# Queueing the sums of weights behind the low parts that precede them

## The chip, the cores and the metric

The kernel runs on one core of a Trainium2 chip. A core has a matrix engine, TensorE (PE in the profile), three engines for elementwise work, VectorE (DVE), ScalarE (ACT) and GpSimd (POOL), and a queue engine, SyncE (SP), that issues most transfers from HBM. Each engine works through its own instructions in program order and waits on semaphores for the others. The metric is the time of one execution on the device, in microseconds (us), as the median of several runs.

## The reference

Two layers, each a mixer between two half-step SwiGLU FFNs, over 512 tokens of width 1024, all in float32. The first layer's mixer is a gated linear attention, the second's a stick-breaking attention. The four FFNs are where the change acts.

```python
D_MODEL, SEQ, DEPTH, D_FF = 1024, 512, 2, 2816

def swiglu(h, w_gate, w_up, w_down):
    return (jax.nn.silu(h @ w_gate) * (h @ w_up)) @ w_down

def reference(x, ffn1_norm, ...):
    for i in range(DEPTH):
        x = x + 0.5 * swiglu(rmsnorm(x, ffn1_norm[i]), ffn1_w_gate[i], ffn1_w_up[i], ffn1_w_down[i])
        h = rmsnorm(x, mix_norm[i])
        ...
        x = x + y.astype(x.dtype)
        x = x + 0.5 * swiglu(rmsnorm(x, ffn2_norm[i]), ffn2_w_gate[i], ffn2_w_up[i], ffn2_w_down[i])
    return rmsnorm(x, final_norm)
```

## The kernel before

**Products in three.** Every operand of a matrix product is split into two parts that PE takes at full speed: a high part, which ScalarE makes by a cast (`wh` for weights, L126), and a low part, which VectorE makes by subtracting the high part from the original (`wl`, L127). One float32 product is then three on PE: high by high, low by high, high by low. For an activation the two parts are called `hh` and `hl`, `nh` and `nl`, `th` and `tl` (L788, L789).

**Blocks of seven products.** Most of the FFNs' products are done in two-by-two blocks with seven block products in place of eight. `seven` (L667) does it for the gate and up projections, `seven_down` (L333) for a part of the down projection. The scheme needs sums of weight blocks: four VectorE additions per block of weights, `s12` and `s34`. In `seven` they are L677 and L678 (`s12`) and L683 and L684 (`s34`), 72 of each; in `seven_down` they are L353, L354, L360 and L361, 16 of each. A sum is itself a weight: it gets a high and a low part.

**Entries, views, splits.** The weights that a step needs are an `Entry`: units of a chunk of raw weights (`raw`, `rawd`), a view of it, and a body, a generator that issues the PE work. A seven-product block is two entries: the first has two raw blocks (`ax`, a11 and the one that goes with b21) and `s12`, the second has `s34` and the raw block a22. `Entry.view` loads the chunk and calls the view: for a raw block that is a slice without an instruction, for a sum it issues the two VectorE additions. `Entry.split` then issues, for each unit, the cast L126 and the subtraction L127. `Feed.start` runs ahead of the entry i that begins: it splits entries i to i+2, views entries up to i+3, and loads the chunks up to i+5.

**Who decides the order.** The instructions are traced in the order of that program, and a scheduler then places them on each engine's queue; `tc.issue_after(x)` makes the instructions traced inside it come later than x in the queue. It adds an order, not a wait.

**What follows the products.** In `seven`'s two bodies PE fills the banks `ps_w`, `ps_q` and `ps_z`. ScalarE copies intermediate sums out (`z` L718, `o1` L721, `o0` L724, `u3` L736), VectorE adds (L737, L740), and in the up projection multiplies by the gate (L707). The products L707 from `ps_z` and `ps_w` also empty those banks. The result is cut into `hh` (L788) and `hl` (L789), the inputs of the down projection.

**The down projection.** An FFN's 11 columns of 256 hidden features come in six groups; groups 1 and 3 go through `seven_down`, in two parts each, 0 and 1, so there are four such blocks in an FFN and 16 in all. Part 0 follows right on the last up pair of its group. Its first body does the products a11 by b11 into `ps_w`, copies them into `ps_z` (L387, ScalarE), then t1 into `ps_q`, t2 on top of `ps_w`, b21 on top of `ps_z`, and adds each into the residual `x` on VectorE (L375). The second body adds t3 on top of `ps_w`, which therefore waits until L375 has added the former content of `ps_w` into x0 and x1.

**Buffers.** The low parts `wl` rotate over four buffers, and so do the high parts and the sums; a low part waits until PE has used the one whose place it takes. The raw weights have two.

Of the kernel before, what the change touches and what calls it, by code (L numbers as in the profile page):

```python
# [10 lines left out]
F32 = mybir.dt.float32  # L11
# [4 lines left out]
ALU = mybir.AluOpType  # L16
# [16 lines left out]
def decoder(ctx: ExitStack, tc: tile.TileContext, a: dict, out: bass.AP):  # L33
    nc = tc.nc
# [59 lines left out]
    class Entry:  # L94
# [7 lines left out]

        def view(self):

            if self.views is None:
                self.views = [view(ch.load()) for ch, view, _, _ in self.units]
            return self.views

        def split(self):
            if self.W is None:  # L110
                self.W = []
                for r, (_, _, n, m) in zip(self.view(), self.units):
                    few = n * m < 1024
                    if few:

                        h = st["few"].tile([P, n * m + NEAR], F32R, tag="vh", bufs=1, name="wh")[:, NEAR:]
                        l = st["few"].tile([P, n * m + 64 - NEAR], F32R, tag="vl", bufs=1, name="wl")[:, : n * m]
                    else:
                        h, l = (
                            wp.tile([P, n * m + 64], F32R, tag="w" + t, bufs=4, name="w" + t)[  # L120
                                :, self.place : self.place + n * m
                            ]
                            for t in "hl"
                        )
                    h, l = (t.rearrange("p (n m) -> p n m", m=m) for t in (h, l))
                    st["cut"] = nc.scalar.copy(h, r).ins  # L126
                    nc.vector.tensor_tensor(out=l, in0=r, in1=h.bitcast(F32), op=ALU.subtract)  # L127
                    self.W.append((h, l))
                    if self.lead and len(self.W) == 1:


                        first = wp.tile([P, P], F32R, tag="w1", bufs=1, name="w1")
                        with tc.issue_after(st["cut"]):
                            nc.scalar.copy(first, r[:, 0, 0:P])
                        self.first = first
# [323 lines left out]
    st = {}  # L459
# [1278 lines left out]
```

## Time and profile before

| | |
|---|---|
| median of 3 runs | 1837.13 us (1836.43 to 1837.6) |
| the profiled execution | 1839.01 us |
| its span | 1837.2 us |
| granted TensorE clock, mean | 0.998 |
| DVE instructions | 2509 |

A row of groups in the profile gives line, engine, operation, the tile written and the tiles read, their shapes and the count, then the total busy time in us and the mean of one in ns, then the idle time just before and what ended it. A row of the timeline gives the start in us from the start of the span, the length in us, and the instruction; idle time before it, with what ended it, stands in brackets. A row of the waits gives who waited for whom, the total, the number of times and the longest, in us. A row of windows gives a stretch, its length and the busy time (and instructions) of PE, PE's weight loads, DVE, ACT and POOL, then the granted clock of TensorE as a share of the full one, and the share and rate of the DMA.

Consecutive short instructions of an engine overlap a little in the records: the distance from start to start is what one of them takes from the engine's time, and it is shorter than the length in the row.

### The profile page before, as it was taken

What the parts mean: (1) busy time and instruction counts of PE and PEld (TensorE: products, weight loads), DVE (VectorE), ACT (ScalarE), POOL (GpSimd) and SP (SyncE); (2) the same over time, 40 slices, a digit from 0 to 9 for tenths busy, and PEclk for the clock granted to TensorE, in tenths of its full rate; (3) what the DMA queues carried; (4) which work ended last, traced back from release to release, by engine and by line L of the source; (5) the groups of instructions that cost most, each with busy time, mean ns of one, the idle gap of its engine ahead of it and who ended that gap; (6) DMA issues with size and microseconds to landing.
All of it is one profiled execution on the core that took longest, in us unless ns stands there. A gap on an engine that the chain in (4) does not pass through costs nothing. (4 is left out here: it accounts for less than half of the span.)

```text
span 1837.2 us, 30777 instructions
## 1 busy us (share of the span) xinstructions
PE 1821.0 (99%) x12476; PEld 1657.2 (90%) x12476; DVE 1530.1 (83%) x2509; ACT 1068.4 (58%) x1842; POOL 8.7 (0%) x20
## 2 busy tenths in 40 slices
PE   8999999999999999999999999999999999999998
PEld 7999999889888899999889999998888788999997
DVE  8999797776787989888798988976878769898885
ACT  6556565444555556555565555645878855565554
POOL 0000000100000000000000000000000000000000
PEclk9999999999999999999999999999999999999999
DMA  5333324221223232323233232322221222333331
GB/s 161 118 124 116 103 93 139 79 69 49 68 69 115 92 111 97 127 93 115 75 121 107 91 125 92 119 86 85 70 70 58 69 92 92 115 106 113 104 104 69
DMA packets 177649, 179.20 MB, mean 98 GB/s; under 512 B 4130, under 2 KB 168020, under 8 KB 177508
## 3 DMA queue, kind: packets, MB, share of 16 engines
q1 hardware_dynamic: 176800, 176.18, 30.2%
q8 instruction: 97, 1.59, 0.4%
q0 software_dynamic: 608, 1.05, 0.2%
q14 instruction: 44, 0.36, 0.1%
q10 hardware_dynamic: 100, 0.03, 0.0%
HBM read 175.17 MB, written 2.10 MB: 96 GB/s over the span
## 5 line engine op out<-in xcount | busy, mean ns | idle before, releaser
L127 DVE TENSOR_TENSOR wl<-raw,wh 128x1024 fp32r<-128x1024 f32 x242 | 256.0, 1061 | 88.0 <-ACT wh L126 46.6
L126 ACT CAST wh<-raw 128x1024 fp32r<-128x1024 f32 (+1 forms) x242 | 223.0, 922 | 157.4 <-PE ps_f L66 35.7
L127 DVE TENSOR_TENSOR wl<-s,wh 128x1024 fp32r<-128x1024 f32 x176 | 214.0, 1219 | 40.4 <-PE ps_z L694 38.5
L694 PE MATMUL ps_w<-th,wh 128*128 128x256 f32 x864 | 239.0, 277 | 0.3
L694 PE MATMUL ps_w<-tl,wh 128*128 128x256 f32 x864 | 238.7, 276 | 0.0
L694 PE MATMUL ps_w<-th,wl 128*128 128x256 f32 x864 | 238.7, 276 | 0.0
L126 ACT CAST wh<-s 128x1024 fp32r<-128x1024 f32 x176 | 184.9, 1050 | 82.8 <-DVE s L684 27.7
L66 PE MATMUL ps_f<-xh,wh 128*128 128x512 f32 x432 | 172.5, 399 | 0.0
L66 PE MATMUL ps_f<-xl,wh 128*128 128x512 f32 x432 | 169.3, 392 | 0.0
L66 PE MATMUL ps_f<-xh,wl 128*128 128x512 f32 x432 | 168.9, 391 | 0.0
L694 PEld LDWEIGHTS ps_w<-th,wh 128*128 128x128 f32 x864 | 162.2, 188 | 0.9 <-ACT ps_z L718 0.9
L694 PEld LDWEIGHTS ps_w<-th,wl 128*128 128x128 f32 x864 | 162.4, 188 | 0.0
L66 PE MATMUL ps_d<-hh,wl 128*128 128x512 f32 x416 | 162.2, 390 | 0.0
L66 PE MATMUL ps_d<-hh,wh 128*128 128x512 f32 x416 | 162.2, 390 | 0.0
L694 PEld LDWEIGHTS ps_w<-tl,wh 128*128 128x128 f32 x864 | 162.2, 188 | 0.0
L66 PE MATMUL ps_d<-hl,wh 128*128 128x512 f32 x416 | 161.8, 389 | 0.0
L126 ACT CAST wh<-rawd 128x1024 fp32r<-128x1024 f32 (+1 forms) x84 | 81.5, 971 | 96.7 <-PE ps_d L66 45.0
L127 DVE TENSOR_TENSOR wl<-rawd,wh 128x1024 fp32r<-128x1024 f32 (+1 forms) x84 | 93.2, 1118 | 20.7 <-PE ps_z L694 11.5
L324 DVE SCALAR_TENSOR_TENSOR x<-ps_d,x 128x512 f32<-128x512 f32 x120 | 80.9, 686 | 21.4 <-PE ps_d L66 21.0
L66 PEld LDWEIGHTS ps_f<-xl,wh 128*128 128x128 f32 x432 | 81.1, 188 | 17.3
L66 PEld LDWEIGHTS ps_f<-xh,wl 128*128 128x128 f32 x432 | 81.3, 188 | 15.6
L66 PEld LDWEIGHTS ps_f<-xh,wh 128*128 128x128 f32 x432 | 81.3, 188 | 15.4
(348 smaller groups left out, 5279.8 us busy)
## 6 DMA issues: line engine op xcount, KB each, us to landing
raw<-in_ffn_w_gate_dram SPq DMA_DIRECT2D x43, 1024.0 KB, 5.3
raw<-in_ffn_w_up_dram SPq DMA_DIRECT2D x43, 1024.0 KB, 5.7
rawd<-in_ffn_w_down_dram SPq DMA_DIRECT2D x84, 512.0 KB, 3.6
raw<-in_gla_w_in_dram SPq DMA_DIRECT2D x12, 1024.0 KB, 5.4
raw<-in_sb_w_in_dram SPq DMA_DIRECT2D x16, 512.0 KB, 3.8
raw<-in_gla_w_out_dram SPq DMA_DIRECT2D x4, 1024.0 KB, 5.0
raw<-in_sb_w_in_dram SPq DMA_DIRECT2D x4, 1024.0 KB, 5.2
raw<-in_sb_w_out_dram SPq DMA_DIRECT2D x4, 1024.0 KB, 5.0
```

The source lines that it names most:

```text
L66: st["pe"] = nc.tensor.matmul(ps, l, r, start=first, stop=last).ins
L126: st["cut"] = nc.scalar.copy(h, r).ins
L127: nc.vector.tensor_tensor(out=l, in0=r, in1=h.bitcast(F32), op=ALU.subtract)
L324: nc.vector.scalar_tensor_tensor(out=xs[k], in0=ps, scalar=0.5, in1=xs[k], op0=ALU.mult, op1=ALU.add)
L694: st["pe"] = nc.tensor.matmul(o, l_, r_, start=first and j + n == 0, stop=j == 3 and n == 2, skip_group_check=True).ins
```

## The change

`Entry.view` issues its additions under an `issue_after` on the last low part that was traced before, and `split` keeps that instruction. The first entries have no low part ahead of them and are left as they were. Two blank lines come in, so that the lines after `view` have numbers greater by two in the kernel after.

```diff
         def view(self):
 
+
             if self.views is None:
-                self.views = [view(ch.load()) for ch, view, _, _ in self.units]
+                with tc.issue_after(st["low"]) if "low" in st else ExitStack():
+                    self.views = [view(ch.load()) for ch, view, _, _ in self.units]
             return self.views
...
                     st["cut"] = nc.scalar.copy(h, r).ins
-                    nc.vector.tensor_tensor(out=l, in0=r, in1=h.bitcast(F32), op=ALU.subtract)
+                    st["low"] = nc.vector.tensor_tensor(out=l, in0=r, in1=h.bitcast(F32), op=ALU.subtract).ins
                     self.W.append((h, l))
```

The number of instructions on each engine and what they compute are the same in both kernels.

## The prediction

> **What bounds the kernel now.** I read the page first: the busy times, then its chain of work that ended last.
>
> ```profile
> span 1837.2 us, 30777 instructions
> ...
> PE 1821.0 (99%) x12476; PEld 1657.2 (90%) x12476; DVE 1530.1 (83%) x2509; ACT 1068.4 (58%) x1842; POOL 8.7 (0%) x20
> ...
> PE ps_w L694 3%; PE ps_d L66 2%; PE ps_q L694 1%; PE ps_bt L66 1%; PE ps_w L369 1%; PE ps_z L694 1%; PE ps_q L369 0%; PE ps_z L369 0%; PE ps_T L1451 0%; ACT xf L1480 0%; ACT ps_bt L1471 0%; DVE x L1462 0%; DVE rq L502 0%; DVE rv L497 0%; ACT ry L499 0%
> ```
>
> PE is busy for 99% of the span and heads the chain. An edit to VectorE (DVE) can therefore act in two ways only: it takes away some of PE's short waits, or it makes new ones. Next come the waits, PE's and then DVE's.
>
> ```profile
> PE ps_q L369 <- DVE o L707: 1.4, 1, 1.4
> PE ps_w L369 <- ACT ps_z L387: 1.2, 2, 0.7
> ...
> DVE wl L127 <- PE ps_z L694: 90.7, 39, 3.8
> ...
> DVE s L677 <- DMA raw<-in_ffn_w_gate_dram: 7.5, 12, 1.9
> ...
> DVE s L677 <- DMA raw<-in_ffn_w_up_dram: 5.0, 5, 2.4
> ```
>
> The two PE rows are all that PE waits for inside the four FFNs, 2.6 us. DVE waits far longer: its low parts (wl, L127) wait 90.7 us for PE to free the buffer they write, and 17 times a sum at the head of its queue waits for its weights to land. The third view is the busy time by stage, for the four FFNs, the only stages that hold sums.
>
> ```profile
> 24.00:318.00 294.00, 293.84 (x2217) 278.66 (x2216) 262.26 (x430) 167.31 (x287) 0.00 (x0) 1.00 0.34 108
> ...
> 630.00:900.00 270.00, 267.75 (x2090) 257.07 (x2089) 232.73 (x379) 150.20 (x259) 0.00 (x0) 0.99 0.33 106
> 925.00:1225.00 300.00, 299.31 (x2235) 283.65 (x2234) 264.72 (x432) 171.81 (x292) 0.00 (x0) 1.00 0.33 103
> 1530.00:1800.00 270.00, 269.88 (x2113) 259.06 (x2112) 239.25 (x389) 153.55 (x267) 0.53 (x1) 1.00 0.34 110
> ```
>
> The columns are length, then PE, PE loads, DVE, ACT and POOL, the granted clock, and DMA. PE idles 3.2 us in all there (0.16, 2.25, 0.69 and 0.12), and the clock is whole but for 0.99 in the second FFN. DVE is busy for 86 to 89%: not the bound, yet with little room to catch up when its order turns bad.
>
> **The change part by part.** Nothing is added or removed: 72 + 16 pairs of entries keep their four sums each.
>
> ```profile
> L677 DVE TENSOR_TENSOR s<-raw 128x512 f32<-128x512 f32 x72 | 49.5, 687 | 12.6 <-DMA raw<-in_ffn_w_gate_dram 7.5 <-DMA raw<-in_ffn_w_up_dram 5.0
> ...
> L353 DVE TENSOR_TENSOR s<-rawd 128x512 f32<-128x512 f32 x16 | 11.0, 686 | 0.0
> ```
>
> So only places move. A sum is now queued behind the last low part traced before it. Before, sums ran while a low part waited for PE; now they run after it, on the far side of other DVE work that stood behind the same low part. In most pairs of the gate and up products this costs nothing: what then follows the sums has room. Where four sums land just ahead of something PE is about to need, it costs. I found such a spot at part 0 of each seven-product down projection (L333 on), where the last up pair's ends and the down products meet: groups 1 and 3 of every FFN, eight places. The instruction orders of the two built programs there, in the line numbers of before:
>
> ```
> before: L737 o1, L677 sum, L740 o0, L707 o1, L707 o0, L707 o1<-ps_w, L127 raw, L127 rawd, L789 hl, L789 hl, L375 x4 x5 x0 x1
> after:  L737 o1, L740 o0, L707 o1, L707 o0, L127 raw, L789 hl, L127 rawd, L677 sum, L707 o1<-ps_w, L678 sum, L683 sum, L789 hl, L684 sum, L375 x4 x5 x0 x1
> ```
>
> The sum that leaves the front is that of a later pair; the four that come in had run well before, while a low part waited. Now the times, for group 3 of the first FFN, from the timeline (start, length).
>
> ```profile
> 253.51 0.42 DVE L737 TENSOR_TENSOR o<-u,o 128x256 f32<-128x256 f32 x1
> 253.85 0.69 DVE L677 TENSOR_TENSOR s<-raw 128x512 f32<-128x512 f32 x1
> 254.46 0.42 DVE L740 TENSOR_TENSOR o<-ps_q,o 128x256 f32<-128x256 f32 x1
> 254.79 0.75 DVE L707 TENSOR_TENSOR o<-o,o 128x256 f32<-128x256 f32 x2
> 255.46 0.42 DVE L707 TENSOR_TENSOR o<-ps_w,o 128x256 f32<-128x256 f32 x1
> 255.79 1.22 DVE L127 TENSOR_TENSOR wl<-raw,wh 128x1024 fp32r<-128x1024 f32 x1
> 256.92 0.68 DVE L127 TENSOR_TENSOR wl<-rawd,wh 128x512 fp32r<-128x512 f32 x1
> 257.53 1.29 DVE L789 TENSOR_TENSOR hl<-o,hh 128x512 fp32r<-128x512 f32 x2
> 258.73 0.75 DVE L375 SCALAR_TENSOR_TENSOR x<-ps_q,x 128x256 f32<-128x256 f32 x2
> ...
> 254.99 0.62 ACT L126 CAST wh<-rawd 128x512 fp32r<-128x512 f32 x1 [0.31 <-PE ps_w L694]
> 255.57 1.14 ACT L788 CAST hh<-o 128x512 fp32r<-128x512 f32 x2
> ...
> 256.83 0.28 PE L369 MATMUL ps_q<-hh,wh 128*128 128x256 f32 x1
> ```
>
> From start to start a 128x512 sum takes 0.60, a 128x256 operation 0.33, the low part of raw 1.13, of rawd 0.61, an hl 0.60. After: L740 starts at 253.84 (the sum ahead of it is gone), the two L707 at 254.17 and 254.51, the raw low part at 254.85, hl at 255.98 (ACT casts hh ahead of wh in the new order, 0.62 each from 254.95, so neither holds it up), the rawd low part at 256.58, the first sum at 257.19, and the L707 on ps_w at 257.79, to end at 258.21. PE's second ps_q product, which started at 256.83, writes the bank that this L707 reads: it starts 1.4 us late. Here x0 (three further sums behind) comes just in time for the then later t3 products.
>
> In other places the bank is free, and the x0 add is what comes late. Group 1 of the first FFN:
>
> ```profile
> 141.92 0.74 DVE L375 SCALAR_TENSOR_TENSOR x<-ps_w,x 128x256 f32<-128x256 f32 x2
> ...
> 142.75 0.28 PE L369 MATMUL ps_w<-nh,wh 128*128 128x256 f32 x1
> ```
>
> The x0 add starts at 141.92 and takes 0.42, so its margin before t3's product at 142.75 is 0.4 us. Four sums come in ahead of it and one leaves: 3 x 0.60 = 1.8 us later, a stall of 1.4 us. Both mechanisms give 1.4; the orders at the other six places are the same, and I take the same price: 8 x 1.4 = 11.2 us. Bounds for one stall: 0, if a cover that I miss holds, and 2.4, the four sums with no cover at all. I take the worked value, since both walks meet there.
>
> The gain is where a sum waited for its DMA in front of work that PE needed.
>
> ```profile
> 850.63 0.42 DVE L737 TENSOR_TENSOR o<-u,o 128x256 f32<-128x256 f32 x1
> 853.45 0.69 DVE L677 TENSOR_TENSOR s<-raw 128x512 f32<-128x512 f32 x1 [2.41 <-DMA raw<-in_ffn_w_up_dram]
> ...
> 855.07 0.42 DVE L707 TENSOR_TENSOR o<-ps_w,o 128x256 f32<-128x256 f32 x1
> ...
> 855.54 0.38 PE L369 MATMUL ps_q<-hh,wh 128*128 128x256 f32 x1 [1.43 <-DVE o L707]
> ...
> 856.23 0.28 PE L369 MATMUL ps_q<-hl,wh 128*128 128x256 f32 x1
> 856.65 0.39 PE L369 MATMUL ps_w<-hh,wh 128*128 128x256 f32 x1
> ...
> 850.00:870.00 20.00, 18.43 (x124) 17.23 (x123) 16.82 (x32) 7.96 (x13) 0.00 (x0) 0.91 0.28 88
> ...
> 746.53 0.39 PE L369 MATMUL ps_w<-hh,wh 128*128 128x256 f32 x1 [0.55 <-ACT ps_z L387]
> ...
> 1043.78 0.39 PE L369 MATMUL ps_w<-hh,wh 128*128 128x256 f32 x1 [0.69 <-ACT ps_z L387]
> ```
>
> With the sum behind, L740 follows L737 at 850.96; then two L707, a rawd low part, an hl, a second low part (0.33 + 0.33 + 1.13 + 0.60 + 0.61, by the rows above), and the L707 on ps_w ends near 854.7 instead of 855.49: PE resumes 0.77 us earlier. The gap before 856.65 (0.3) goes too, since ACT then copies z ahead of its second hh. Right after, the clock is halved: 0.91 over 20 us is 1.8 us, and with a smaller stall I expect this dip gone. That is 2.8; with the waits at 746.53 (0.55) and 1043.78 (0.69), the recovery is 4.0 us. Its bounds are 0 and, idle plus clock, 3.2 + 1.8 = 5.0.
>
> Sum: 11.2 - 4.0 = +7.2 us. Against the profiled execution's own 1839.0 us (1837.2 of span, 1.8 around it) that is 1846.2. That execution lies 1.9 above the median of the runs, 1837.1, so the median goes to 1844.3.
>
> A new stall could also bring a dip of the clock, worth 1.8 us each by the row above.
>
> ```profile
> 852.95:856.36 3.41, 1.98 (x17) 1.73 (x15) 2.91 (x6) 1.18 (x3) 0.00 (x0) 1.00 0.00 0
> ...
> 744.85:748.26 3.41, 2.86 (x22) 2.50 (x21) 3.41 (x7) 1.75 (x5) 0.00 (x0) 1.00 0.13 20
> ```
>
> Two stretches of the same length: with PE idle for 1.43 us a dip followed, with 0.55 us none did (its clock stays 1.00, as does the FFN but for this spot). A stall of 1.4 us is at the upper of the two; but the one at 855.54 had a second gap right behind it, and mine stand alone. I take no dip and keep eight, 14.4 us, as the far bound.
>
> The Trainium skill speaks to this: in TensorE: Matmul & The Clock Gate, section "HAM oscillation — how this bites in real kernels", the rule is that only PE gaps above some 3.4 us drop the clock. By that rule no 1.4 us stall costs clock and the sum stays at +7.2; the trace does not agree, since 0.91 follows a gap of 1.43 us.
>
> **The rivals.** First, dips: the stalls come as forecast and most halve the clock. For it, the 855.54 row; against it, that gap's companion. Time: 1844.3 + 8 x 1.8 = 1858.7, with half of them 1851.5.
>
> Second, covered: the stalls are half as long, because DVE, 11 to 14% idle in an FFN, arrives at these places earlier than in the rows. For it, the 90.7 us of waits of low parts; against it, the walk starts from where DVE really stood at 253.51, and its nine rows follow one another without a gap. Time: 1837.1 + 5.6 - 4.0 = 1838.7, no change that can be told.
>
> Third, the other side, faster: moving DMA-bound sums out of the head of DVE's queue is all that counts. Its place is the 853.45 sum and the two z copies, its price -4.0 us, 1833.1. From an average of 0.5 us a stall downward (8 x 0.5 = 4.0) there is no loss, and under 0.04 us (4.0 - 3.7, over 8) the kernel is measurably faster. For it: these are the only waits of PE that the trace names. Against: the x0 margin of 0.4 us cannot hold 1.8.
>
> That the change does nothing is out: the two programs' DVE orders differ at every pair.
>
> **How the numbers follow.** A difference of 0.2% (3.7 us) is about what can be told from no change here. The forecast, +4 to +11 us without many dips, gets 0.52; dips at several or most stalls 0.17; covered 0.18; faster 0.13. So slower 0.69, same 0.18, faster 0.13, and 1844.3 is predicted. The range runs from 1836, a little under the covered case, to 1858, close to all dips; it leaves out the faster case and little else. The likeliest case's own range is 1841 to 1848.
>
> **What would show it.** Right: in the waits, PE ps_q L369 waiting for L707 and PE ps_w L369 waiting for DVE x L375, about eight waits of some 1.4 us, two in each FFN; the windows' idle time of PE in the FFNs up from 3.2 us to some 12; the sums' own DMA waits (L677) no longer ahead of L740; the wait at 746.53 and the dip after 855.54 gone. A clock under 1.00 in an FFN window would speak for dips. Wrong: no L375 or L707 among PE's waits, or new waits of PE for wl (L127), whose room in the pairs I called free.

## The result, and the profile after

| | before | after |
|---|---|---|
| median of 6 runs each | 1836.78 us (1834.62 to 1838.58) | 1848.58 us (1846.47 to 1849.77) |
| ratio | | 1.0064, 95% interval 1.0051 to 1.0077 |
| the profiled execution, its span | 1839.01 us, 1837.2 us | 1847.70 us, 1845.9 us |

The change costs 11.8 us, 0.64%. The forecast was 7.2 us slower. The two profiled spans differ by 8.7 us only: the profiled execution of before lay 2.2 us above the median here, that of after 0.9 us below. This matters further down.

First the page and PE's waits of the kernel after, then the queue engine's waits (its lines carry numbers greater by two, for one blank line and the line of the `with` that came in).

```profile
span 1845.9 us, 30813 instructions
...
PE 1819.5 (99%) x12476; PEld 1655.4 (90%) x12476; DVE 1538.0 (83%) x2509; ACT 1066.1 (58%) x1842; POOL 8.7 (0%) x20
...
PE ps_q L371 <- DVE o L709: 6.9, 6, 1.3
PE ps_w L371 <- DVE x L377: 5.3, 5, 1.3
...
PE ps_q L371 <- ACT o L706: 1.0, 2, 0.7
...
SPq L91 <- DVE s L363: 36.6, 16, 2.9
```

Engine shares tell nothing: PE is still at 99%, with the same work. The waits tell more. Of before's two rows inside the FFNs, 2.6 us, one has grown to 6.9 and the other, on the z copies, is gone; in its place PE waits 5 times for the x0 add, and twice, 1.0 us in all, for a silu of ScalarE's (L706). VectorE's 12.5 us of sums that wait for their weights are gone too, as the prediction had it. The last row was not there before: the transfers now wait for L363, the last sum of a down projection block.

The windows of the four FFNs:

```profile
24.00:318.00 294.00, 291.22 (x2189) 275.64 (x2188) 261.48 (x424) 166.59 (x286) 0.00 (x0) 1.00 0.34 105
630.00:900.00 270.00, 266.25 (x2096) 255.88 (x2095) 237.01 (x381) 149.72 (x259) 0.00 (x0) 1.00 0.34 107
925.00:1225.00 300.00, 296.78 (x2212) 280.70 (x2210) 263.16 (x426) 169.45 (x289) 0.00 (x0) 1.00 0.33 102
1530.00:1800.00 270.00, 266.50 (x2061) 254.59 (x2060) 241.25 (x389) 151.68 (x266) 0.53 (x1) 1.00 0.35 108
```

PE's idle time in them is 2.8, 3.8, 3.2 and 3.5 us, 13.3 together against 3.2 before, and the clock is 1.00 in each: no dip. The place that the prediction walked through, group 3 of the first FFN, in the timeline after:

```profile
255.55 0.42 DVE L739 TENSOR_TENSOR o<-u,o 128x256 f32<-128x256 f32 x1
255.88 0.42 DVE L742 TENSOR_TENSOR o<-ps_q,o 128x256 f32<-128x256 f32 x1
256.22 0.75 DVE L709 TENSOR_TENSOR o<-o,o 128x256 f32<-128x256 f32 x2
256.88 1.22 DVE L129 TENSOR_TENSOR wl<-raw,wh 128x1024 fp32r<-128x1024 f32 x1
258.02 0.68 DVE L791 TENSOR_TENSOR hl<-o,hh 128x512 fp32r<-128x512 f32 x1
258.62 0.68 DVE L129 TENSOR_TENSOR wl<-rawd,wh 128x512 fp32r<-128x512 f32 x1
259.23 0.68 DVE L679 TENSOR_TENSOR s<-raw 128x512 f32<-128x512 f32 x1
259.83 0.41 DVE L709 TENSOR_TENSOR o<-ps_w,o 128x256 f32<-128x256 f32 x1
...
260.30 0.39 PE L371 MATMUL ps_q<-hh,wh 128*128 128x256 f32 x1 [1.27 <-DVE o L709]
...
144.88 0.39 PE L371 MATMUL ps_w<-nh,wh 128*128 128x256 f32 x1 [1.27 <-DVE x L377]
```

From L739 to the L709 on ps_w it is 259.83 - 255.55 = 4.28 us; the walk had 257.79 - 253.51 = 4.28. The wait shows as 1.27 in the bracket, but the product before 260.30 started at 258.75 and products start 0.11 apart, so PE lost 1.43 us by the starts, and the next product comes 0.11 later than usual. What PE lost is given by the starts from here on; a figure in a bracket or a row of the waits is some 0.17 us smaller. The second row of PE is group 1, with the x0 add in the same part. By the starts of the products, the eight places lost 1.43 or 1.44 us each: four on the bank, four on x0.

### The profile page after: what moved, and what is told of

It is laid out like the page before. It is cut to its first block, busy times and chain, and to the rows that moved or that the text cites. A ratio compares the mean times of both kernels' runs of the same rounds, so it can differ in the third digit from the quotient of the medians.

```text
span 1845.9 us, 30813 instructions
## 1 busy us (share of the span) xinstructions
PE 1819.5 (99%) x12476; PEld 1655.4 (90%) x12476; DVE 1538.0 (83%) x2509; ACT 1066.1 (58%) x1842; POOL 8.7 (0%) x20
## 5 line engine op out<-in xcount | busy, mean ns | idle before, releaser
L696 PE MATMUL ps_w<-tl,wh 128*128 128x256 f32 x864 | 238.6, 276 | 0.0
L696 PE MATMUL ps_w<-th,wh 128*128 128x256 f32 x864 | 238.6, 276 | 0.0
L696 PE MATMUL ps_w<-th,wl 128*128 128x256 f32 x864 | 238.6, 276 | 0.0
L696 PEld LDWEIGHTS ps_w<-th,wh 128*128 128x128 f32 x864 | 162.3, 188 | 0.0
L696 PEld LDWEIGHTS ps_w<-th,wl 128*128 128x128 f32 x864 | 162.2, 188 | 0.0
L696 PEld LDWEIGHTS ps_w<-tl,wh 128*128 128x128 f32 x864 | 162.2, 188 | 0.0
```

Of the source, the lines that this page charges most:

```text
L696: st["pe"] = nc.tensor.matmul(o, l_, r_, start=first and j + n == 0, stop=j == 3 and n == 2, skip_group_check=True).ins
```

## The experiments

Each kernel marks the entries of the sums and takes the edge for some of them only. The mark is 0 for the pair that comes right after part 0 of a down block, eight pairs in all, 2 for the down projection's own sums, in one kernel split into 2 and 3 for parts 0 and 1. The core of every edit is the condition. These kernels have some more lines: their L683, L684, L713, L700 and L796 are L679, L680, L709, L696 and L791 of the kernel after, L371 and L377 are the same.

### The kernel before, again

> The kernel before, unchanged, for a second profile of it. My theory of the eight stalls puts the lost time at 8 x 1.54 = 12.3 us of new waits and takes the recovery of 4.0 us that I forecast for what one profile showed: if PE's wait of 1.43 us at 855.54 and the dip of the clock behind it were those of one execution only, this profile lacks them, its span is near 1834 to 1835 us, and there is nothing to recover there. The rival, that they belong to the kernel: the same waits and a clock of 0.91 in that 20 us window stand here again, span near 1837.

1837.36 us (11 runs), ratio 0.9997 (0.9988 to 1.0006); the profiled span was 1835.5. The window of the prediction's largest recovery, in this profile, and PE's waits inside the FFNs:

```profile
850.00:870.00 20.00, 20.00 (x150) 18.91 (x150) 18.78 (x35) 9.71 (x16) 0.00 (x0) 1.00 0.33 107
...
PE ps_w L369 <- ACT ps_z L387: 1.3, 3, 0.7
PE ps_q L369 <- DVE o L707: 0.7, 1, 0.7
...
PE ps_q L369 <- ACT o L704: 0.5, 1, 0.5
```

In this window PE does not idle at all and the clock is whole. The wait of 1.43 us at that place and the dip stand in the first profile only. The waits add up to as much as there (2.5 us here, 2.6 there), but at other places (0.8 us lost at 1617.77, 0.9 at 1039.75); what is missing here is the dip. It seems to be rare: the granted clock was 0.998 in the first profiled execution, and 0.999 or more in 48 of the 55 runs of the kernel before that were timed beside the experiments. A recovery of 2.8 us at that place was to be had in the first execution, not in the median one. The waits on the z copies stand in both profiles (1.2 and 1.3 us).

### The eight pairs alone, and all but the eight

```diff
-                with tc.issue_after(st["low"]) if "low" in st else ExitStack():
+                with tc.issue_after(st["low"]) if "low" in st and self.site == 0 else ExitStack():
```

> The order edge only for the pair of sums whose views come right after part 0 of each seven-product down projection, 8 pairs of 88; all other sums as before. My theory (these eight places are the loss, 1.43 us of wait and 0.11 us of a slower second product each): about 12.3 us over before, 1849 us, with PE waiting 6 times for the ps_w product and 5 or more times for the x0 add, 1.3 us each. The rival that the loss is spread over all sums (DVE later everywhere, raw and rawd transfers later): a tenth of the loss, 1838 us. The rival that late down-projection weights make most of it: no change, 1837 us.

1854.78 us, ratio 1.0097 (1.0083 to 1.0111): 17.6 us over the kernel before on the same chip (1837.15), more than the whole change costs with 88 pairs moved.

```profile
PE ps_q L371 <- DVE o L713: 6.2, 5, 1.3
PE ps_w L371 <- DVE x L377: 5.1, 4, 1.3
PE ps_q L700 <- DVE x L377: 4.5, 4, 1.1
...
267.04 0.68 DVE L683 TENSOR_TENSOR s<-raw 128x512 f32<-128x512 f32 x1
...
267.98 0.68 DVE L684 TENSOR_TENSOR s<-s,raw 128x512 f32<-128x512 f32 x1
...
270.31 0.75 DVE L377 SCALAR_TENSOR_TENSOR x<-ps_w,x 128x256 f32<-128x256 f32 x2
...
270.78 0.38 PE L700 MATMUL ps_q<-th,wh 128*128 128x256 f32 x1 [1.13 <-DVE x L377]
```

The first two rows are the eight waits, with one more. The third is new: seven or ten us behind four of these places, PE waits for the x add that frees the bank of its next ps_q. There two sums of the following pair stand in front of that add, and DVE now comes there later; in the kernel before, one stood there and the other had run at 253.85. With the full change both are queued behind the add, and the row is absent. The size of the eight was right; I had not expected the moved pair to push what follows.

```diff
+                with tc.issue_after(st["low"]) if "low" in st and self.site != 0 else ExitStack():
```

> The edge for all sums but those of the eight pairs right after part 0. My theory: the eight waits of 1.4 us are gone and the time falls by 12.3 us to about 1836 us; the waits of 0.4 to 1.4 us at part 1, where the down-projection weights now land late, stay. The rival of a loss spread over all sums: 1847 us. The rival that the late transfers of down-projection weights are the larger part: 1843 us or more.

1836.07 us (11 runs), ratio 0.9991 (0.9982 to 1.0000). Against the full change, 1848.58, 12.5 us are gone (12.9 when each is set against its own runs of before); 8 x (1.43 + 0.11) = 12.3. Without the edge on these eight pairs the loss is gone. What is left on PE's list stands at part 1:

```profile
PE ps_q L371 <- DVE o L713: 1.4, 2, 0.9
...
PE ps_w L371 <- DVE x L377: 0.3, 1, 0.3
```

### The gate and up sums without the eight, and the down sums alone

```diff
+                with tc.issue_after(st["low"]) if "low" in st and self.site not in (0, 2) else ExitStack():
```

> The edge only for sums of the gate and up projections, and not for the eight pairs right after part 0; the down projection's own sums are placed as before, so that its raw buffer comes free as early as before. My theory: no wait at part 0, no late weights at part 1, and the sums that waited for their transfer at the head of the queue moved away: 1833 to 1836 us, as fast as before or up to 4 us faster. The rival that moving any sum behind the low parts costs: over 1840 us.

1838.34 us, ratio 1.0007 (0.9998 to 1.0016): not faster, and my reason failed. PE waited for the L713 that empties ps_w six times; four of the waits stand at part 0, cost 1.38 or 1.39 us each and have no sum ahead of that L713:

```profile
PE ps_q L371 <- DVE o L713: 6.2, 6, 1.2
...
254.39 1.22 DVE L129 TENSOR_TENSOR wl<-raw,wh 128x1024 fp32r<-128x1024 f32 x1
255.52 0.69 DVE L796 TENSOR_TENSOR hl<-o,hh 128x512 fp32r<-128x512 f32 x1
256.13 0.69 DVE L129 TENSOR_TENSOR wl<-rawd,wh 128x512 fp32r<-128x512 f32 x1
256.73 0.42 DVE L713 TENSOR_TENSOR o<-ps_w,o 128x256 f32<-128x256 f32 x1
```

The L713 on ps_w comes behind two low parts and an hl, while in the kernel before it came ahead of them. The scheduler put it there. The edges so act twice: they move the sums, and they change the scheduler's choice for work that has no edge. At the four places of the ps_q kind the low parts and hl in front of L709 (1.13 + 0.60 + 0.61 us) weigh more than the one sum (0.60) that I spoke of. They do not give 1.38 us alone: at the place shown DVE begins this stretch (L743, L739 in the kernel after) 2.8 us before the waiting product was due, where it was 3.3 us with the full change, and that makes up for the missing sum.

```diff
+                with tc.issue_after(st["low"]) if "low" in st and self.site == 2 else ExitStack():
```

> The edge only for the down projection's own sums (16 blocks). My theory: it delays the last reader of the raw down weights, so that the queue engine waits for that sum 16 times, the next weights land later, and PE waits at part 1 in some FFNs, 0.3 to 1 us each, 2 to 4 us together, offset by nothing: 1838 to 1841 us, with no wait of 1.4 us at part 0. The rival that late down weights are hidden: 1837 us.

1839.75 us, ratio 1.0015 (1.0006 to 1.0024), 2.9 us over its own before (1836.84).

```profile
PE ps_q L700 <- DVE x L377: 3.2, 4, 1.0
PE ps_q L371 <- ACT o L710: 1.1, 2, 0.9
...
SPq L91 <- DVE s L363: 42.3, 16, 2.9
```

The queue engine waits for L363 16 times, 42.3 us in all. The size is as expected, the place only in part: 1.1 us of PE's waits are at part 1, and 3.2 us (4 times) again for the x add that frees the bank of the next ps_q.

### The down weights earlier

In the changed kernel the raw down weights have two buffers, and the block's last sum frees one. Issues on the queue engine, before (the first two rows) and after:

```profile
844.53 0.37 SPq L91 DMA_DIRECT2D rawd<-in_ffn_w_down_dram  x1
845.30 0.37 SPq L91 DMA_DIRECT2D raw<-in_ffn_w_up_dram  x1
```

```profile
848.88 0.37 SPq L91 DMA_DIRECT2D raw<-in_ffn_w_up_dram  x1
851.41 0.37 SPq L91 DMA_DIRECT2D rawd<-in_ffn_w_down_dram  x1
...
856.12 1.05 ACT L128 CAST wh<-rawd 128x1024 fp32r<-128x1024 f32 x1 [1.60 <-DMA rawd<-in_ffn_w_down_dram]
...
860.02 0.38 PE L371 MATMUL ps_q<-hh,wh 128*128 128x256 f32 x1 [1.20 <-DVE o L709]
```

Their order is reversed: the down weights leave 2.5 us behind the up weights, and not 0.8 us ahead of them. The cast for part 1 then waits 1.60 us for them to land. PE lost 1.37 us there, at 860.02, at the same product as at 855.54 in the first profile of before. So the wait for the raw weights that the change took away was partly replaced by a wait for the down weights. The late landing is not all of it, since the L709 on ps_w also stands behind two low parts and an hl here: the kernel of the last experiment, in which the down weights go out first again (848.88, the up weights at 849.65), still loses 0.83 us at this product, and the changed kernel loses 0.83 us at the same place of the fourth FFN (1775.80), where the cast waits for no transfer. That leaves some 0.5 of the 1.37 us to the landing. The next kernel leaves the edge off the eight pairs and off the sums of part 1, and half of the moved issues go back to their place.

```diff
+            e.site = 2 + part
...
+                with tc.issue_after(st["low"]) if "low" in st and self.site not in (0, 3) else ExitStack():
```

> The edge for all sums but those of the eight pairs right after part 0 and those of the part-1 blocks of the down projection. On each VectorE queue the multiply that empties the ps_w bank stands ahead of the low parts at part 0 as before, and half of the moved transfers on the queue engine stand where they stood before. My theory: the gain of moving sums that waited for their transfer, without the waits at part 0 and with fewer at part 1: 1833 to 1836 us. The rival that the gain was one execution's chance: 1837 us, as before.

1833.07 us, ratio 0.9981 (0.9971 to 0.9990): it is below both kernels, by 3.8 us (its own before, 1836.84) and 15.5 us.

```profile
PE ps_q L371 <- DVE o L713: 1.1, 2, 0.7
...
SPq L91 <- DVE s L363: 20.5, 8, 2.6
...
842.70 0.37 SPq L91 DMA_DIRECT2D rawd<-in_ffn_w_down_dram  x1
```

The down weights go out ahead of the up weights again at this place, the queue engine waits 8 times in place of 16, and the kernel is 3.0 us below the one without the eight pairs, 2.7 when each is set against its own runs of before (1836.84 and 1837.15); the intervals of the two ratios overlap. The two kernels differ in the part-1 sums' place on VectorE too, so that this gain is not shown to be the transfers' alone.

### More sums in the same place

```diff
                 nc.vector.tensor_tensor(out=s[:, 0:4], in0=t[:, 0:4, P:], in1=t[:, 4:8, P:], op=ALU.add)
+                for _ in range(3 if mark == 0 else 0):
+                    nc.vector.tensor_tensor(out=s[:, 0:4], in0=t[:, 0:4, P:], in1=t[:, 4:8, P:], op=ALU.add)
```

> As the kernel with the edge on the eight pairs alone (1854.8 us), with the first sum of each of these eight pairs done twice, one more 128x512 addition in the same place. The theory that x0 is late by the sums ahead of it: each of the eight places loses one sum more, 0.60 us, so 8 x 0.60 = 4.8 us, 1859.6 us. The rival that a margin behind them takes it up: under 2 us more.

> The same with the first sum done four times, three more additions at each of the eight places. The theory of x0: 8 x 1.80 = 14.4 us more than the kernel with the edge on the eight pairs alone, 1869.2 us, with the clock at 1.00 in the FFNs. The rival that a wait of this length halves the clock for 3.4 us each time: up to another 8 x 1.8 = 14.4 us, 1883 us, with windows at 0.9 around the places.

1860.23 us (5.5 over the kernel with the eight pairs alone, 4.8 expected) and 1873.66 us (18.9 over it, 14.4 expected without dips). At the four x0 places PE's loss went from 1.44 to 2.04 and 3.24 us, 0.60 per sum to the hundredth. At the four others it stayed at 1.43 or 1.44 for the bank and a second wait for x0 came behind it, of 0.4 to 0.5 and 1.6 to 1.7 us, so that x0 was just in time there, as the walk had it. The waits and the clock of the kernel with three more:

```profile
PE ps_w L371 <- DVE x L377: 18.1, 8, 3.1
...
145.57 0.38 PE L371 MATMUL ps_w<-nh,wh 128*128 128x256 f32 x1 [3.07 <-DVE x L377]
...
145.60:152.50 6.90, 6.90 (x46) 6.90 (x47) 5.27 (x10) 3.18 (x5) 0.00 (x0) 0.75 0.00 0
845.10:852.00 6.90, 6.90 (x46) 6.90 (x47) 5.26 (x10) 3.18 (x5) 0.00 (x0) 0.75 0.00 0
1063.50:1070.40 6.90, 6.90 (x46) 6.90 (x47) 5.26 (x10) 3.16 (x5) 0.00 (x0) 0.75 0.01 2
1770.80:1777.70 6.90, 6.89 (x45) 6.89 (x46) 5.21 (x10) 3.48 (x6) 0.00 (x0) 0.75 0.01 2
262.90:269.80 6.90, 5.50 (x44) 5.29 (x45) 6.90 (x14) 2.97 (x5) 0.00 (x0) 1.00 0.23 76
```

Each window starts where a wait ended. A clock of 0.75 over 6.9 us is 1.7 us lost; it follows each of the four waits of 3.24 us. By the products it is 1.6 us: from 145.57 to PE's next wait it takes 8.91 us, and 7.31 from the same product in the kernel with the eight pairs alone. It does not follow the paired waits (1.43 and 1.57 us, the last row). The longer waits and four dips add to some 20.5 us against the 18.9 measured; the waits at part 1, which differ from execution to execution (1.6 us in this profile, 3.0 in that of the eight pairs alone), can be the rest. With one more sum, four waits of 2.04 us, the dip followed one:

```profile
1053.93 0.39 PE L371 MATMUL ps_w<-nh,wh 128*128 128x256 f32 x1 [1.87 <-DVE x L377]
...
1053.90:1060.80 6.90, 6.87 (x46) 6.87 (x47) 5.25 (x10) 2.53 (x5) 0.00 (x0) 0.75 0.01 2
```

### The changed kernel, again, and without the down sums

> The changed kernel, unchanged, for a second profile and for a comparison on one chip. My theory: the eight waits of 1.4 us at part 0 stand again to within 0.05 us, the waits at part 1 differ by some tenths, 1848 to 1849 us. The rival that the eight are chance, as those at 855 us of the kernel before were: other places.

1848.39 us, ratio 1.0064 (1.0051 to 1.0077). The eight waits stand at the same products and again at 1.43 to 1.44 us each; the ones at part 1 differ (1.15 us at 858.38 where the first profile had 1.37).

```diff
+                with tc.issue_after(st["low"]) if "low" in st and self.site != 2 else ExitStack():
```

> The edge for all sums of the gate and up projections, the eight pairs after part 0 among them; the down projection's own sums as before. My theory: the eight waits stay, and the down weights land earlier by what that gave elsewhere (the kernel with half of the transfers back in place against the one without: 1833.1 against 1836.1 us), so about 3 us less than the changed kernel, 1845.6 us. The rival that the loss at part 0 needs the down projection's sums too: 1837 us. The rival that the transfers do nothing while PE is late anyway: 1848.6 us.

1846.37 us, ratio 1.0056 (1.0042 to 1.0069); the eight waits stay at 1.43 or 1.44 us. That is 2.0 us below the changed kernel of the same chip, where about 3 were expected; the two intervals overlap, so this step is the least certain of the set. The profiles agree with it: the queue engine waits for L363 no more, and PE loses 1.4 us at part 1, against 3.9 and 2.9 us in the two profiles of the changed kernel.

## Why the prediction was right, and which term was off

**The eight places: right.** Both mechanisms, their count, their places and their size (1.4 us forecast, 1.43 to 1.44 measured) held in two profiles, and the x0 kind followed the number of sums when more were put in; taking the edge off these eight pairs takes the whole loss away. The term is 12.3 instead of 11.2 us: 0.03 more for each, and the 0.11 us by which the product behind a wait is late. The account of the ps_q kind was incomplete: the walk counts the low parts and the hl ahead of L709, yet the prediction lays the stall to sums that land there, while with no sum there the same products waited 1.38 us, because the low parts and the hl stood ahead of L713 and DVE came there later.

**"The recovery is 4.0 us": mis-sized.** Without the eight pairs the change gains 1.1 us (0 to 3.3 by the interval) and not 4.0. Part of the forecast gain came: no wait on the z copies is left in the two profiles of the changed kernel. Two causes of the rest show. The recovery was read from a single execution, and 2.8 of it came from a wait and a dip that a second profile of the same kernel lacks. In effect the dip was also counted twice: the sum takes off its 1.8 us as recovery and then another 1.9 us to come from that execution to the median, while the second profile, of an execution at the median (1837.36 us), holds no dip. From one profiled execution to the other the change cost 8.7 us, and 12.3 - 8.7 = 3.6 us came back, close to the 4.0; from median to median it is 12.3 - 11.8 = 0.5 us.

The second cause lies at part 1. The step from "the sum no longer waits at the head of the queue" to "PE resumes earlier" left out the transfers: the down block's sums are the last readers of the raw down weights, and moving them held back the next transfer. With PE resuming 0.77 us earlier, the walk leaves 0.66 of the wait of 1.43 us in the bracket; the kernel with the down sums in place shows 0.66 there, the changed kernel 1.20 and 0.99. The walk's order was also priced at the one place where the first profile had a wait; in the fourth FFN it made a new one of 0.83 us. The prediction priced VectorE's order and never priced the queue engine's, although the change moves what releases its buffers. 12.3 - 1.1 = 11.2 us agrees with the measured 11.8 to within the runs' spread.

**Dips: rightly left out.** All eight waits of 1.43 to 1.44 us left the clock at 1.00 here and in the repeat. The far bound of the range rested on a wait that had a second gap behind it; the prediction set it apart for that, and a wait of the same length, 1.60 us by the starts, that stood alone (1800.08, with three more sums) brought no dip either. The rule of the Trainium skill (TensorE: Matmul & The Clock Gate, section "HAM oscillation — how this bites in real kernels"), that only gaps above some 3.4 us count, gave the right sum here. It is not what the chip did in the experiments: 3.24 us halved the clock four times of four, 2.04 us once of four.

**Covered and faster: wrong** for the changed kernel: the stalls came at full size, and the margin of 0.4 us did not hold the sums. Yet the faster rival describes the kernel without the eight pairs and the part-1 sums, 0.19% below before.

## What to carry to other kernels

An order that suits most of 88 places can lose everything at the eight where a bank, or an accumulation, waits for work queued behind it: look at what follows the moved instructions at each kind of place, not at the engine's busy share. A moved instruction that is the last reader of a buffer moves a transfer as well, so the queue that refills the buffer belongs in the sum. A recovery that is read from waits in one execution needs a second profile of the same kernel before it is counted, and must not be taken off again on the way to the median. Here waits made by program order came back to the hundredth of a microsecond; those at which a transfer came late did not.

## What the hardware did that I had not expected

The clock's answer to idle time showed no sharp edge at one length of wait. By the starts, none of the single waits of 1.43 to 1.44 us brought a dip in the windows read for it, one of four at 2.04 us did and all four at 3.24 us, each worth 1.6 to 1.7 us. Two waits of 1.43 and 1.57 us, with 3.6 us of work between them, brought none, while 1.60 and 0.31 us close together at 855.54 and 856.65 did (the brackets there say 1.43 and 0.14). What decides at 2.04 us is open.
